# Splitting the blocks of the next down-product later and its weights earlier in a Strassen-scheduled encoder layer

## The chip, the cores and the metric

The kernel runs on one core of a Trainium2 chip. The metric is the device time of one launch in microseconds (us).

## The reference, cut to what matters

One layer of a hybrid streaming encoder (recurrent and gated mixers, output projection, then a gated feed-forward part) over 1024 prompt frames and 64 sample frames, 1088 columns in all. The change lies in the last product of the layer, the down projection of the feed-forward part, and in the normalisation and residual add behind it:

```python
    hn2 = rmsnorm(x, g_pre2)
    up = hn2 @ w_up
    upc, new_ffn = causal_dwconv(up, ffn_prev, w_conv_f, b_conv_f)
    f = (jax.nn.gelu(upc[..., :D_FF]) * upc[..., D_FF:]) @ w_down
    x = x + rmsnorm(f, g_post2)
```

D_MODEL is 1024 and D_FF is 3072. The frames lie along the free axis, the features along the 128 partitions.

## The kernel before

The kernel first runs the mixers, the output projection and the up projection, and spends its last quarter in the down projection. Every matrix product is made of three passes: an operand is split into a high part (written by ACT, `hi`) and a low part (the operand less its high part, by DVE, `lo`), and high by high, high by low and low by high are added up in PSUM. So each operand costs one ACT and one DVE instruction before TensorE can use it.

The down projection is done by a Strassen scheme: seven half-size products (`DOWN`), whose operands are sums of quarters. Each product has six steps (`down_step`, 48 matmuls of 272 columns each), so steps are numbered 0 to 41. Step n needs its own weights (one tile of 128x1024, high and low) and two of the six gated blocks of its product: steps 0 and 3 of a product use blocks 0 and 1, steps 1 and 4 blocks 2 and 3, steps 2 and 5 blocks 4 and 5. A step takes the first of its two blocks at its start and the second a quarter of the step later. I number blocks through, 6 to a product, as `bload` and `bmake` do.

- `bload(b)` (L977) loads a block of 128x1088 from DRAM on the SP queue, as tile `graw`; `bmake(b)` splits it into `gh` (L143, ACT) and `gl` (L145, DVE).
- `wload(n)` (L998) loads the one or two weight quarters of step n on the SP queue, as `wraw`; `wmake(n)` first takes their difference where there are two (L1008, DVE; products 2, 3 and 6, so steps 12 to 23 and 36 to 41) and then splits it into `whi` (L143) and `wlo` (L145).
- `down_step(n)` issues the matmuls (L1069) into PSUM tiles `dps`. In the third step of each half product DVE adds the sums to the accumulators `facc` (L1078), on ACT for the first product (L1086), and for some products their squares are summed (`ssqt`, L221 and L222).
- The last product (steps 36 to 41) is done over two column ranges (`COLS2`, r = 0 and 1), each over all six weight sets, into tiles `lps`. Its first range, as long as three steps, takes the weight sets in turn, half a step's length each; set 41 is first wanted 2.5 steps after its start, and block 41 after 2.15.
- `finish` normalises a finished range of columns: `rstd_head` (matmuls `st`, L196, then L187 on DVE and L188 on POOL), `rstd_tail` (matmuls `bp`, L208, and a copy on ACT), then eight scalings on DVE (L1121). For the first half of the columns the result is added to the residual in DRAM by POOL's DMAs; for the last two ranges the residual is loaded by `load_xn` (L1108, SP queue) and added on DVE (L1126, and L1144 in `finish_last`).

All these tiles but PSUM's come from one pool of 47 buffers of a row of 1096 words. A high or low part can be written only when an earlier tile's readers, mostly matmuls of an earlier step, are done with its buffer. The order of instructions on each engine is fixed when the program is built: the text order above, as a scheduler with priorities places it. Engines and the SP queue work through their rows in that order, so an instruction that waits holds back all rows behind it on its engine.

Of the kernel before, what the change touches and what calls it, by code (L numbers as in the profile page):

```python
# [41 lines left out]
NDS = 6 * len(DOWN)  # L42
# [25 lines left out]
def layer_kernel(ctx: ExitStack, tc, xT, w_fm, w_v, w_o, w_up, w_down, w_g, w_s, par, bc, yT, small, vn_out):  # L68
# [9 lines left out]
    def bank_tile(name):  # L78
        return mmp.tile([P, 512], F32, tag="mm", name=name)
# [3 lines left out]
    def big_tile(dt=F32, shape=(P, TW), name="t"):  # L83
        return big.tile(list(shape), dt, tag="t", name=name)

    def tmp_tile(w, name="d"):
        return tmp.tile([P, 288], F32, tag="d", name=name)[:, :w]
# [54 lines left out]
    def split(hi, lo, src, scale=None):  # L142
        nc.scalar.activation(hi, src, AF.Copy, scale=1.0 if scale is None else scale)  # L143
        if scale is None:
            nc.vector.tensor_tensor(lo, src, hi.bitcast(F32), op=ALU.subtract)  # L145
        else:
            nc.vector.scalar_tensor_tensor(lo, src, scale, hi.bitcast(F32), op0=ALU.mult, op1=ALU.subtract)
# [93 lines left out]
    def pcols(i):  # L241
        return slice(i * PC, min(i * PC + PC, T))
# [71 lines left out]
    for k in range(KD):  # L314
        xh.append(big_tile(F32R, name="xh")[:, :T])
        xl.append(big_tile(F32R, name="xl")[:, :T])
        if k == 0:
# [3 lines left out]
            for i in range(3):  # L321
                n = pcols(i).stop - pcols(i).start
# [12 lines left out]
    for i in range(3):  # L335
        n = pcols(i).stop - pcols(i).start
# [6 lines left out]
    s = [big_tile(name="s")[:, :T] for _ in range(4)]  # L343
# [275 lines left out]
    def run(gen):  # L619
        for _ in gen:  # L620
            pass
# [349 lines left out]
    bq, braw, wq, wraw = {}, {}, {}, {}  # L971
    sd = drp.tile([2, 6, P, 1024], F32, tag="sd", name="sd")

    def bload(n):
        if n < NDS:
            braw[n] = big_tile(name="graw")[:, :T]
            nc.sync.dma_start(braw[n], bd[n // 6, n % 6].rearrange("p a t -> p (a t)"))  # L977

    def bmake(n):
        if n < NDS:  # L980
            bq[n] = big_tile(F32R, name="gh")[:, :T], big_tile(F32R, name="gl")[:, :T]
            split(*bq[n], braw.pop(n))

    def w_index(n):
        i = n % 6
        return i if n < NDS - 6 else i % 2 * 3 + i // 2

    def wload(n):
        if n >= NDS:
            return  # L990
        p, i = n // 6, w_index(n)
        a11, a12, a21, a22 = (w_down[r, c, i] for r in range(2) for c in range(2))
        s1, s2 = sd[0, i], sd[1, i]
        wraw[n] = []
        for src in {"A11": (a11,), "S2": (s1, a11), "S3": (a11, a21), "A22": (a22,), "A12": (a12,),
                    "S1": (s1,), "S4": (a12, s2)}[DOWN[p][1]]:
            t = big_tile(shape=(P, 1024), name="wraw")
            nc.sync.dma_start(t, src)  # L998
            wraw[n].append(t)

    def wmake(n):
        if n >= NDS:
            return
        p, i = n // 6, w_index(n)
        raw = wraw.pop(n)
        src = raw[0]
        if len(raw) == 2:
            nc.vector.tensor_tensor(src, src, raw[1], op=ALU.subtract)  # L1008
        if DOWN[p][1] == "S2":
            nc.gpsimd.dma_start(sd[1, i], src)  # L1010
        wq[n] = big_tile(F32R, (P, 1024), name="whi"), big_tile(F32R, (P, 1024), name="wlo")
        split(*wq[n], src)
# [9 lines left out]
    for j in range(NPRE, NF):  # L1022
# [7 lines left out]
        i = j - NPRE - 2  # L1030
# [9 lines left out]
    late.pop()()  # L1040
    opb.clear()
    wmake(2)
    bmake(5)
    wload(4)
    wmake(3)
    bload(6)

    ssqt = []
    gens2 = []
# [1 line left out]
    def tick2():  # L1051
        if gens2 and next(gens2[0], 0) == 0:
            gens2.pop(0)

    def facc_cols(m, lo, hi):
        return facc[m][:, lo:hi]

    def sq_add(m, lo, hi, eng=None):
        if not ssqt:
            ssqt.append(big_tile(name="ssqt")[:, :T])  # L1060
        add_sq(ssqt[0][:, lo:hi], facc_cols(m, lo, hi), m == (0 if lo < HT else 4), eng)

    def down_mm(dst, cols, n, kg, k, mi, first, last):
        hi, lo = wq[n]
        bh, bl = bq[n // 6 * 6 + kg * 2 + k // 2]
        o = k % 2 * HT
        for q, (wt, at) in enumerate(((hi, bh), (hi, bl), (lo, bh))):
            for ps, (a, b) in zip(dst, cols):
                nc.tensor.matmul(ps, wt[:, k * 256 + mi * P:k * 256 + (mi + 1) * P], at[:, o + a:o + b],  # L1069
                                 start=(first and k == 0 and q == 0), stop=(last and k == 3 and q == 2))  # L1070
# [33 lines left out]
    def load_xn(cols):  # L1104
        w = cols.stop - cols.start
        xn = [big_tile(name="xn")[:, :4 * w].rearrange("p (m t) -> p m t", m=4) for _ in range(2)]
        for g in range(2):
            nc.sync.dma_start(xn[g], yT[:, 4 * g:4 * g + 4, cols])  # L1108
        return xn

    def finish(cols, xn=None):
        w = cols.stop - cols.start
        head = rstd_head(ssqt[0][:, cols], D)
        yield
        yield
        rr = tmp_tile(w, name="rrf")
        rstd_tail(head, rr)
        yield
        for m in range(KD):
            f = facc[m][:, cols]  # L1120
            nc.vector.scalar_tensor_tensor(f, f, pv("g_post2", m), rr, op0=ALU.mult, op1=ALU.mult)  # L1121
            if xn is None:
                nc.gpsimd.dma_start(yT[:, m, cols], f, accum_op=ALU.add)
            else:
                x = xn[m // 4][:, m % 4, :]
                nc.vector.tensor_tensor(x, x, f, op=ALU.add)  # L1126
                if m % 4 == 3:
                    nc.sync.dma_start(yT[:, m - 3:m + 1, cols], xn[m // 4])
            if m % 2 == 1:
                yield  # L1130

    def scale_f(m, cols):
        f = facc[m][:, cols]
        nc.scalar.activation(f, f, AF.Copy, scale=pv("g_post2", m))
# [14 lines left out]
    def down_step(n):  # L1149
        p, mp, kg = n // 6, n % 6 // 3, n % 3  # L1150
        for mi in range(2):
            m = 2 * mp + mi
            if kg == 0:
                dps[m] = [bank_tile("dps")[:, :HC] for _ in CC]
            for k in range(4):
                down_mm(dps[m], CC, n, kg, k, mi, kg == 0, kg == 2)
            if kg == 2:
                down_evac(p, m, dps.pop(m))
            tick2()
        if mp == 1:  # L1160
            for b in range(2):
                del bq[p * 6 + 2 * kg + b]
        del wq[n]

    dps = {}
    n0 = NDS - 6
    for n in range(n0):
        if n == n0 - 6:
            for c in COLS1:
                gens2.append(finish(slice(*c)))  # L1170
        down_step(n)
        wmake(n + 4)
        if n < n0 - 6:
            bmake(n + 6)
            bload(n + 7)
        elif n == n0 - 6:
            bload(n0 + 1)
            bmake(n0)
            bload(n0 + 2)
            bmake(n0 + 1)  # L1180
        elif n < n0 - 1:
            bload(n + 8)
            bmake(n + 7)
        wload(n + 5)
        if n == 0:
            while todo:
                run(todo.pop(0))
        if n == 1:
            nc.gpsimd.dma_start(small, sm)
    wmake(n0 + 4)  # L1190
    wload(n0 + 5)
    for r, (lo, hi) in enumerate(COLS2):
        cols = slice(lo, hi)
        w = hi - lo
        loc = [(lo - HT, hi - HT)]
        xn = load_xn(cols)
        pss = [bank_tile("lps")[:, :w] for _ in range(4)]

        def mm(m, kg):
            for k in range(4):  # L1200
                down_mm([pss[m]], loc, n0 + 2 * kg + m // 2, kg, k, m % 2, kg == 0, kg == 2)
            tick2()

        if r == 0:
            for kg in range(2):
                for m in range(4):
                    mm(m, kg)
                if kg == 0:
                    wmake(n0 + 5)
        else:  # L1210
            for m in range(4, KD):
                scale_f(m, cols)
        for m in range(4):
            for kg in range(2 if r == 0 else 0, 3):
                mm(m, kg)
            f = facc_cols(m, lo, hi)
            with tc.high_priority(offset=PRI):
                nc.vector.tensor_tensor(f, pss[m], f, op=ALU.add)
                if r == 1 and m == 3:
                    more = tmp_tile(w, name="sq")  # L1220
                    nc.scalar.activation(more, f, AF.Square)
                else:
                    sq_add(m, lo, hi)
                    if r == 1:
                        scale_f(m, cols)
        if r == 0:
            gens2.append(finish(cols, xn))
# [80 lines left out]
```

## Time and profile before

| | |
|---|---|
| median of 3 runs | 1160.79 us (1159.71 to 2815.52) |
| the profiled execution's own time | 1158.54 us |
| its span, first to last instruction | 1156.8 us |
| busy: PE, DVE, ACT, POOL | 97%, 73%, 46%, 14% |
| start of the down projection in the span | 866.71 us |

The profiled execution's own time is its span and 1.7 us around it. One of the three runs, at 2815.52 us, is far off the other two. Times in the rows are microseconds from the start of the span; "mean ns of one" is the duration of one instruction.

### The profile page before, as it was taken

The page shows a single profiled execution, that of the slowest core. Times are in us where ns is not written, and L with a number is a line of the kernel's source. Part 1 is how long each engine was busy: PE and PEld are TensorE (multiplying, and loading weights), DVE is VectorE, ACT ScalarE, POOL GpSimd, SP SyncE. Part 2 cuts the span into 40 slices and gives each one's busy share as a digit, 9 for nine tenths or more (in the row PEclk, how much of TensorE's full clock was granted, in tenths as well). Part 3 has the DMA queues.
Part 4 walks back from the last instruction along what each step waited for, and adds up shares of the span by engine and source line. Part 5 has one row for each costly group of instructions (what it writes and reads, how often), then busy time and mean ns, then how long its engine had stood idle before and what let it go on. Part 6 is the DMA issues. An engine that isn't in the chain of part 4 may idle for free.

```text
span 1156.8 us, 20691 instructions
## 1 busy us (share of the span) xinstructions
PE 1125.6 (97%) x8420; PEld 1104.3 (95%) x8420; DVE 845.1 (73%) x1415; ACT 535.3 (46%) x923; POOL 163.3 (14%) x277
## 2 busy tenths in 40 slices
PE   7999999999999999999999999999999998999995
PEld 6799999999998999999999999999999998999885
DVE  7567776856687898887787787887889355744766
ACT  7213846545445546544544544444466232523421
POOL 0210001010000122222112021021022000001310
PEclk9999999999999999999999999999999999999988
DMA  8110111221333125465342142142168689455952
GB/s 317 37 42 19 37 55 37 66 84 53 97 116 117 37 84 159 141 191 125 94 141 95 47 141 95 47 141 95 47 220 324 230 292 331 133 188 180 270 133 78
DMA packets 53615, 148.61 MB, mean 128 GB/s; under 512 B 5520, under 2 KB 23440, under 8 KB 53424
## 3 DMA queue, kind: packets, MB, share of 16 engines
q1 hardware_dynamic: 39648, 114.57, 29.4%
q0 software_dynamic: 13104, 32.04, 9.2%
q8 instruction: 66, 1.08, 0.4%
q10 hardware_dynamic: 768, 0.69, 0.2%
q14 instruction: 29, 0.24, 0.1%
HBM read 111.57 MB, written 41.99 MB: 133 GB/s over the span
## 4 chain that ended last, share of the span: by engine, by line
PE 91%; DVE 5%; issue 2%; ACT 1%; DMA 0%; POOL 0%; SPq 0%; POOLq 0%; DVEq 0%; ACTq 0%
PE up L901 40%; PE dps L1069 17%; PE ps L429 12%; PE ops L654 7%; PE pps L769 4%; PE vps L294 3%; PE lps L1069 3%; PE gps L515 1%; PE bp L208 1%; PE sp L386 1%; ACT whi L143 1%; PE st L196 1%; DVE wraw L1008 1%; DVE gl L145 1%; DVE bl L145 0%
## 5 line engine op out<-in xcount | busy, mean ns | idle before, releaser
L901 PE MATMUL up<-bh,wop 128*128 128x272 f32 x2464 | 466.0, 289 | 0.0
L901 PEld LDWEIGHTS up<-bh,wop 128*128 128x128 f32 x2464 | 386.7, 188 | 2.1 <-ACT uraw L916 1.3
L901 PE MATMUL up<-bl,wop 128*128 128x272 f32 x1232 | 354.8, 288 | 0.0
L901 PEld LDWEIGHTS up<-bl,wop 128*128 128x128 f32 x1232 | 231.9, 188 | 0.0
L1069 PE MATMUL dps<-gh,whi 128*128 128x272 f32 x576 | 120.2, 291 | 3.1 <-ACT whi L143 3.0
L1069 PE MATMUL dps<-gl,whi 128*128 128x272 f32 x576 | 120.6, 290 | 1.6 <-DVE gl L145 1.5
L1069 PE MATMUL dps<-gh,wlo 128*128 128x272 f32 x576 | 120.0, 290 | 0.0
L143 ACT ACTIVATE wop<-wsum 128x512 fp32r<-128x512 f32 x88 | 53.3, 628 | 116.8 <-DVE wsum L857 76.3
L145 DVE TENSOR_TENSOR wlo<-wraw,whi 128x1024 fp32r<-128x1024 f32 x70 | 85.1, 1220 | 27.5 <-ACT whi L143 27.2
L143 ACT ACTIVATE whi<-wraw 128x1024 fp32r<-128x1024 f32 x70 | 73.2, 1055 | 67.7 <-DVE wraw L1008 56.4
L1069 PEld LDWEIGHTS dps<-gh,whi 128*128 128x128 f32 x576 | 91.1, 190 | 3.5 <-ACT whi L143 3.3
L1069 PEld LDWEIGHTS dps<-gl,whi 128*128 128x128 f32 x576 | 91.4, 190 | 2.2 <-DVE gl L145 2.2
L916 ACT ACTIVATE uraw<-up 128x272 f32<-128x272 f32 (+2 forms) x220 | 67.9, 344 | 53.8 <-PE up L901 53.5
L1069 PEld LDWEIGHTS dps<-gh,wlo 128*128 128x128 f32 x576 | 91.2, 190 | 0.1
L801 DVE SCALAR_TENSOR_TENSOR yg<-uraw,pt,yg 128x1090 f32<-128x1090 f32 (+1 forms) x48 | 64.8, 1350 | 26.4 <-ACT yg L799 26.4
L922 DVE TENSOR_TENSOR uraw<-up,uraw 128x272 f32<-128x272 f32 (+2 forms) x176 | 58.8, 364 | 32.2 <-PE up L901 29.9
L654 PE MATMUL ops<-yh,whi 128*128 128x272 f32 x256 | 75.1, 293 | 0.0
L654 PE MATMUL ops<-yh,wlo 128*128 128x272 f32 x256 | 73.7, 288 | 0.0
L654 PE MATMUL ops<-yl,whi 128*128 128x272 f32 x256 | 73.6, 288 | 0.0
L429 PE MATMUL ps<-xh,whi 128*128 128x364 f32 (+2 forms) x296 | 69.4, 328 | 0.0
L188 POOL TENSOR_TENSOR rs<-v,mhalf 91x3 f32<-91x3 f32 (+2 forms) x20 | 24.6, 1229 | 308.2 <-DVE v L187 308.2
L429 PE MATMUL ps<-xh,wlo 128*128 128x364 f32 (+2 forms) x296 | 67.7, 324 | 0.0
(219 smaller groups left out, 2181.6 us busy)
## 6 DMA issues: line engine op xcount, KB each, us to landing
wraw<-in_w_up_dram SPq DMA_DIRECT2D x48, 512.0 KB, 4.1
graw<-bd SPq DMA_DIRECT2D x42, 544.0 KB, 5.5
wraw<-in_w_down_dram SPq DMA_DIRECT2D x42, 512.0 KB, 6.3
bd<-yg POOLq DMA_DIRECT2D x36, 272.0 KB, 3.4
wraw<-sd SPq DMA_DIRECT2D x18, 512.0 KB, 5.9
bd<-ta POOLq DMA_DIRECT2D x24, 272.0 KB, 4.2
bd<-tb POOLq DMA_DIRECT2D x24, 272.0 KB, 3.4
wraw<-in_w_fm_dram SPq DMA_DIRECT2D x12, 512.0 KB, 3.6
```

The source lines that it names most:

```text
L143: nc.scalar.activation(hi, src, AF.Copy, scale=1.0 if scale is None else scale)
L145: nc.vector.tensor_tensor(lo, src, hi.bitcast(F32), op=ALU.subtract)
L188: nc.gpsimd.tensor_tensor(out, v[:n[0], :n[1]], mhalf[:n[0], :n[1]], op=ALU.pow)
L294: nc.tensor.matmul(ps[b][:vrows(b), :], a[:, vcols(b)], wt[:, o:o + 512], start=False, stop=(k == KD - 1 and q == 2))
L429: nc.tensor.matmul(ps[c], wt[:, k * P:(k + 1) * P], at[k][:, cols], start=(k == 0 and q == 0), stop=(k == KD - 1 and q == 2))
L654: nc.tensor.matmul(ps, wt[:, i * 256 + mi * P:i * 256 + (mi + 1) * P], a[k, c], start=(first and i == 0 and j == 0), stop=(last and i == 3 ...
L769: nc.tensor.matmul(ps, wt[:, k * P:(k + 1) * P], a[k, c], start=(k == 0 and j == 0), stop=(k == KD - 1 and j == 2))
L801: nc.vector.scalar_tensor_tensor(y[:, d:TG], x[:, :TG - d], tap(2 - d), y[:, d:TG], op0=ALU.mult, op1=ALU.add)
L901: nc.tensor.matmul(dst[c], wt[:, k * P:(k + 1) * P], at[:, fourth(k)], start=(start and k == 0 and q == 0), stop=(k == 3 and q == 2), skip ...
L916: nc.scalar.activation(d, src[c][:, cut], AF.Copy)
L922: nc.vector.tensor_tensor(d, src[c][:, cut], d, op=ALU.add)
L1069: nc.tensor.matmul(ps, wt[:, k * 256 + mi * P:k * 256 + (mi + 1) * P], at[:, o + a:o + b], start=(first and k == 0 and q == 0), stop=(last ...
```

## The change

The order of loads and splits in the down projection is written anew, in a helper `operands_after(n)` that runs behind each step. Weights of step n + 4 (one or two steps more from step 34 on) are split first, and weights are loaded two steps beyond that, in place of one. Blocks of the next product are no longer split one behind each step, six steps ahead (up to step 29), but by a table `B_MAKE`: none behind the second step of a product (block 6 there stands for the next product's first), block 6 behind its third step, 7 and 8 behind its fourth, 9 behind its fifth, 10 behind its sixth, and the last one behind the first step of the next product. A block is loaded one step before it is split, and behind the weight loads of its step. Before step 0, block 5 is no longer split and block 6 no longer loaded. In the last product the weight splits and the last block splits now stand behind its two first thirds, and the residual load of r = 0 behind these matmuls, in place of ahead of them.

```diff
@@ -1040,10 +1040,8 @@
     wmake(2)
-    bmake(5)
     wload(4)
     wmake(3)
-    bload(6)
@@ -1164,36 +1162,39 @@
+    B_MAKE = {2: (6,), 3: (7, 8), 4: (9,), 5: (10,), 0: (5,)}
+
+    def operands_after(n):
+        made = max(wq)
+        up_to = min(n + 4 + max(0, n - n0 + 4) // 2, NDS - 1)
+        while wloaded[0] < min(up_to + 2, NDS - 1):
+            wloaded[0] += 1
+            wload(wloaded[0])
+        for i in range(made + 1, up_to + 1):
+            wmake(i)
+        s = n % 6
+        for b in B_MAKE.get(s, ()):
+            bmake(n - s + b)
+        for b in B_MAKE.get((s + 1) % 6, ()):
+            bload(n + 1 - (s + 1) % 6 + b)
+
+    wloaded = [4]
     for n in range(n0):
...
         down_step(n)
-        wmake(n + 4)
-        if n < n0 - 6:
-            bmake(n + 6)
-            bload(n + 7)
-        elif n == n0 - 6:
-            bload(n0 + 1)
-            bmake(n0)
-            bload(n0 + 2)
-            bmake(n0 + 1)
-        elif n < n0 - 1:
-            bload(n + 8)
-            bmake(n + 7)
-        wload(n + 5)
+        operands_after(n)
...
-    wmake(n0 + 4)
-    wload(n0 + 5)
     for r, (lo, hi) in enumerate(COLS2):
...
-        xn = load_xn(cols)
+        xn = load_xn(cols) if r else None
...
             for kg in range(2):
                 for m in range(4):
                     mm(m, kg)
-                if kg == 0:
-                    wmake(n0 + 5)
+                operands_after(n0 + kg)
+            xn = load_xn(cols)
```

On DVE around the end of product 2, this is the order before. The first row is the weight difference of step 17, `facc` rows are the sums at the end of step 17, and `wraw_10650` belongs to step 18.

```order
L1008 TENSOR_TENSOR wraw_10586<-wraw_10586,wraw_10588 128x1024
L145 TENSOR_TENSOR wlo_10641<-wraw_10586,whi_10640 128x1024
L145 TENSOR_TENSOR gl_10645<-graw_10584,gh_10644 128x1088
L1078 TENSOR_TENSOR facc_10061<-dps_10721,facc_10061 128x272
L1078 TENSOR_TENSOR facc_10061<-dps_10722,facc_10061 128x272
L1078 TENSOR_TENSOR facc_10090<-dps_10747,facc_10090 128x272
L1078 TENSOR_TENSOR facc_10090<-dps_10748,facc_10090 128x272
L1008 TENSOR_TENSOR wraw_10650<-wraw_10650,wraw_10652 128x1024
L145 TENSOR_TENSOR wlo_10708<-wraw_10650,whi_10707 128x1024
L145 TENSOR_TENSOR gl_10712<-graw_10648,gh_10711 128x1088
```

And now on DVE, `wraw_10572` is step 18 and `wraw_10634` step 19, and the `facc` rows are the sums at the end of step 14.

```order
L1008 TENSOR_TENSOR wraw_10572<-wraw_10572,wraw_10574 128x1024
L145 TENSOR_TENSOR wlo_10641<-wraw_10504,whi_10640 128x1024
L1008 TENSOR_TENSOR wraw_10634<-wraw_10634,wraw_10636 128x1024
L1076 TENSOR_TENSOR facc_9857<-dps_10520,facc_9857 128x272
L1076 TENSOR_TENSOR facc_9857<-dps_10521,facc_9857 128x272
L145 TENSOR_TENSOR wlo_10704<-wraw_10572,whi_10703 128x1024
L1076 TENSOR_TENSOR facc_9886<-dps_10546,facc_9886 128x272
L1076 TENSOR_TENSOR facc_9886<-dps_10547,facc_9886 128x272
L145 TENSOR_TENSOR gl_10708<-graw_10644,gh_10707 128x1088
```

The difference and the split for step 18 moved from behind the sums of step 17 to the sums of step 14, three steps earlier.

On DVE at the start of the last product, this is the order before: the split for step 36 (`wlo_11926`), sums and squares of step 35, six scalings of `finish`, and then the difference for step 37 (`wraw_11935`).

```order
L145 TENSOR_TENSOR wlo_11926<-wraw_11848,whi_11925 128x1024
L1078 TENSOR_TENSOR facc_10090<-dps_11970,facc_10090 128x272
L145 TENSOR_TENSOR gl_11932<-graw_11842,gh_11931 128x1088
L222 TENSOR_TENSOR ssqt_10259<-ssqt_10259,sq_12147 128x272
L222 TENSOR_TENSOR ssqt_10259<-ssqt_10259,sq_12150 128x272
L1121 SCALAR_TENSOR_TENSOR facc_10061<-facc_10061,pt_79,rrf_12113 128x272
L1121 SCALAR_TENSOR_TENSOR facc_10090<-facc_10090,pt_79,rrf_12113 128x272
L1121 SCALAR_TENSOR_TENSOR facc_11070<-facc_11070,pt_79,rrf_12113 128x272
L1121 SCALAR_TENSOR_TENSOR facc_11097<-facc_11097,pt_79,rrf_12113 128x272
L1121 SCALAR_TENSOR_TENSOR facc_11260<-facc_11260,pt_79,rrf_12113 128x272
L1121 SCALAR_TENSOR_TENSOR facc_11287<-facc_11287,pt_79,rrf_12113 128x272
L1008 TENSOR_TENSOR wraw_11935<-wraw_11935,wraw_11937 128x1024
```

And now on DVE the sums in the middle of step 35 (the `facc` rows) come behind the splits for steps 38, 39 and 40 (`wlo_12068`, `wlo_12073`, `wlo_12162`). The row `v` is the second `rstd_head`, which waits for `st` matmuls that now stand in the middle of step 34.

```order
L1008 TENSOR_TENSOR wraw_11983<-wraw_11983,wraw_11985 128x1024
L187 TENSOR_SCALAR v_12031<-st_12026 91x3
L1008 TENSOR_TENSOR wraw_12058<-wraw_12058,wraw_12060 128x1024
L145 TENSOR_TENSOR wlo_12068<-wraw_11910,whi_12067 128x1024
L145 TENSOR_TENSOR wlo_12073<-wraw_11983,whi_12072 128x1024
L145 TENSOR_TENSOR gl_12077<-graw_12000,gh_12076 128x1088
L145 TENSOR_TENSOR wlo_12162<-wraw_12058,whi_12161 128x1024
L1076 TENSOR_TENSOR facc_11256<-dps_11927,facc_11256 128x272
L1076 TENSOR_TENSOR facc_11256<-dps_11928,facc_11256 128x272
```

The splits for steps 36 and 37 moved further up still, ahead of the first `finish`; only the one for step 41 is left behind these rows, after the six scalings.

## Rows read from the trace of the kernel before

**Rows 1.** PE's waits from 820 us on: total us, times, longest.

```profile
PE lps L1069 <- ACT whi L143: 4.6, 2, 2.6
PE dps L1069 <- ACT whi L143: 3.0, 1, 3.0
PE bp L208 <- POOL rs L188: 2.0, 2, 1.4
PE dps L1069 <- DVE gl L145: 1.5, 2, 1.0
```

**Rows 2.** Matmuls of L1069 in 10-us stretches: PE busy (count), PEld, PEclk, DMA share, GB/s.

```profile
890.00:900.00 10.00, 10.00 (x83) 10.00 (x82) 1.00 0.77 277
...
950.00:960.00 10.00, 9.42 (x71) 8.76 (x70) 1.00 0.79 297
970.00:980.00 10.00, 6.96 (x54) 6.75 (x54) 0.93 1.00 378
980.00:990.00 10.00, 10.00 (x61) 9.92 (x61) 0.73 0.35 123
1060.00:1070.00 10.00, 8.28 (x64) 7.69 (x62) 1.00 0.42 85
1090.00:1100.00 10.00, 7.06 (x45) 6.42 (x44) 0.90 0.89 272
1100.00:1110.00 10.00, 7.38 (x40) 7.04 (x39) 0.76 1.13 282
1130.00:1140.00 10.00, 8.26 (x64) 7.88 (x63) 1.00 0.01 2
```

**Rows 3.** The chain of waits from 840 us on: start, us, what.

```profile
866.87 72.06 PE dps L1069 x575
...
977.31 1.14 DVE wraw L1008
...
1057.73 0.41 PE st L196 x6
...
1064.29 0.65 PE bp L208 x6
```

**Rows 4.** Timeline of SP from 944 us: the loads for step 18.

```profile
945.50 2.74 SPq L998 DMA_DIRECT2D wraw<-in_w_down_dram  x2
```

**Rows 5.** The page's DMA issues: KB each, median us to landing.

```profile
wraw<-in_w_down_dram SPq DMA_DIRECT2D x42, 512.0 KB, 6.3
```

**Rows 6.** Timeline of DVE, steps 11 to 14: start, us, [idle before <-releaser].

```profile
935.92 0.79 DVE L1078 TENSOR_TENSOR facc<-dps,facc 128x272 f32<-128x272 f32 x2 [8.52 <-PE dps L1069]
...
940.86 1.49 DVE L222 TENSOR_TENSOR ssqt<-ssqt,sq 128x272 f32<-128x272 f32 x4
...
944.61 1.23 DVE L145 TENSOR_TENSOR wlo<-wraw,whi 128x1024 fp32r<-128x1024 f32 x1 [1.12 <-ACT whi L143]
945.75 1.29 DVE L145 TENSOR_TENSOR gl<-graw,gh 128x1088 fp32r<-128x1088 f32 x1
```

**Rows 7.** Timeline of DVE at the start of the last product.

```profile
1091.26 1.49 DVE L1078 TENSOR_TENSOR facc<-dps,facc 128x272 f32<-128x272 f32 x4 [5.60 <-PE dps L1069]
...
1094.19 1.22 DVE L1008 TENSOR_TENSOR wraw<-wraw 128x1024 f32<-128x1024 f32 x1
...
1099.93 2.56 DVE L1121 SCALAR_TENSOR_TENSOR facc<-facc,pt,rrf 128x272 f32<-128x272 f32 x6
1102.41 1.22 DVE L1008 TENSOR_TENSOR wraw<-wraw 128x1024 f32<-128x1024 f32 x1
```

**Rows 8.** Timeline of ACT in steps 0 and 1: the weight split of step 4.

```profile
874.31 1.06 ACT L143 ACTIVATE whi<-wraw 128x1024 fp32r<-128x1024 f32 x1 [0.17 <-DMA wraw<-in_w_down_dram]
```

**Rows 9.** Timeline of DVE in the tail.

```profile
1147.83 0.44 DVE L1126 TENSOR_TENSOR xn<-xn,facc 128x274 f32<-128x274 f32 x1
```

**Rows 10.** Timeline of POOL: the second and third `rs` of `finish`.

```profile
1070.10 4.21 POOL L188 TENSOR_TENSOR rs<-v,mhalf 91x3 f32<-91x3 f32 x1
...
1135.69 0.88 POOL L188 TENSOR_TENSOR rs<-v,mhalf 92x3 f32<-92x3 f32 x1 [29.69 <-DVE v L187]
```

## Prediction

> **What bounds the kernel now.** I read the waits of PE first, then PE's matmuls in stretches of 10 us, then the chain and the timelines of DVE, ACT and SP around the stops. PE is the engine that sets the end: in an undisturbed stretch of the down projection its matmuls follow each other without a pause, 575 in 72.06 us or 125.3 ns each [rows 3], so a step of 48 takes 6.015 us. The reader is to see where it does not run like that. PE waits for a high part of a weight (`whi`) 4.6 us in the last product and 3.0 us at the start of step 18, and for `gl` 1.5 us [rows 1]. The stretches show what that costs: 82 to 83 matmuls of L1069 in ten undisturbed us, but 71 from 950 us, 54 and 61 from 970, 64 from 1060, 45 and 40 from 1090 and 64 from 1130 [rows 2]. The granted clock falls to 0.73 behind the stop of step 18 and to 0.76 behind those of the last product [rows 2], so part of the time stands at the lower of the two levels, 1.2 in place of 2.4 GHz, although PE has work.
>
> Are late loads the reason? No. The two quarters for step 18 were issued from 945.50 us on [rows 4] and such loads land in a median of 6.3 us [rows 5], so they lay there by about 955; their difference began at 977.31 [rows 3]. DVE came late, by its order: the difference stands behind the sums of step 17, and these wait for PE. DVE idles in front of such sums, 8.52 us at 935.92 [rows 6], with splits queued behind them; later it runs difference, `wlo` and `gl` one by one, with 1.12 us of waiting for ACT in each turn [rows 6]. It is the same in the last product: the difference for step 36 begins at 1094.19, behind the sums of step 35, and that for step 37 at 1102.41, behind six scalings of 2.56 us [rows 7], while PE stands.
>
> **Weights split earlier, step 18.** Now this difference and split stand at the sums of step 14. Without stops step n begins at 866.7 + 6.015 n, so those sums come at about 953 to 957 and step 18 begins at 975.0: about 18 us of room in place of none. The stop and the slow clock behind it go. From 970 us two stretches have 115 matmuls in place of 164: 49 times 0.1253 is 6.1 us.
>
> **Blocks split later.** This frees buffers for the weights, but each block comes nearer to its use, and a late one stops PE as 950 us and 1060 us show: 11 and 18 matmuls missing, 1.4 and 2.3 us, of which 1.06 us in the second are the `st` and `bp` matmuls (0.41 and 0.65 [rows 3]) that stay. I go through the nearest places, by DVE's new order. In product 2 the last block `gl` (for step 14 and a quarter, due at 952.7) stands behind the sums of step 11 (at 938.9 plus 0.8), four additions of squares (1.5), two differences, two `wlo` and two `gl`; these six take 1.14 to 1.28 us each, start to start, if ACT is ahead, which it is with one split of 1.06 us [rows 8] for each. That ends at about 948.3, 4.4 us ahead; with ACT's 1.12 us [rows 6] in each of two turns still 2.2 us ahead. In product 0, block 5 is split behind the weights of steps 3 and 4. Before, step 4's `whi` began at 874.31 as its load landed [rows 8]; then come `wlo`, 1.06 us later, or ACT's `gh` (by its width 1.1 us), and DVE's `gl`, 1.28 us: done at about 877.9, and due at step 2.29, 880.5. That is 2.6 us ahead. Other products have 5 us and more. So I take nothing for new stops here, and nothing left of the old: 1.4 and 2.3 less 1.06 us, or 2.6 us, are won.
>
> **The last product.** Splits for sets 36 to 40 now stand ahead of the sums of step 35, so PE finds them at once. The longest thing left is set 41: behind the start of step 36 DVE has four sums (1.49 [rows 7]), two squares (0.8), a `gl` of 1.28, six scalings (2.56), a difference (1.14), ACT's `whi` with its hand-over (1.15), `wlo` and the last `gl`, 10.9 us in all, and block 41 is due 2.15 steps or 12.9 us behind that start. So 2 us ahead, no stop. From 1090 us the stretches lack 79 of 164 matmuls, 9.9 us, of which a `bp` of 0.65 us stays: 9.25 us. At 1130 us 18 are missing, 2.3 us, of which `st` and `bp` keep 1.06: before, `bp` came so soon behind `st` that PE waited for POOL [rows 1], now half a step lies between. That is 1.2 us.
>
> **Loads.** The weight loads that pass the block loads on SP are worth nothing by themselves, since loads lay 20 us unused (above). Their price is bounded by block loads that come later: these go behind one step's weights, at most two loads, and are issued a step ahead of their split. The residual load of r = 0 stands now behind the last block loads, at about 1080 us, and its data are used behind `finish`, in step 40, some 25 us later. It costs nothing; in the tail, one residual addition of r = 0 that stood among the last sixteen operations (0.44 us, of which 0.35 count [rows 9]) goes.
>
> **The sum.** 6.1 + 2.6 + 9.25 + 1.2 + 0.35 is 19.5 us. Against the profiled execution's own 1158.54 us that is 1139.0. I leave 0.5 us for short waits at `st` and `bp`, which I bound by 0 and by the 2.0 us of [rows 1]. The two near runs stand 1.2 and 2.3 us above the profiled execution, so a median should come at 1139.5 + 1.5, or **1141 us**, 1.7% below 1160.79. There is little to win beyond that: with all these gone PE runs through.
>
> **The rivals.**
> *POOL late.* The second `rs` now falls beside five operations of DVE in a row (a difference, three `wlo`, a `gl`), each with two inputs from SBUF, some 5.9 us. The same operation took 4.21 us at 1070 among DVE work and 0.88 us at 1135.69 with DVE nearly idle [rows 10]. If it waits them all out and then takes 0.88 us, it ends 6.8 us behind `v`, and `bp` is due 5.3 us behind `v`: PE stops for 1.5 us, and the time is 1142.5. For it: the 4.21 us. Against: even 4.21 us would fit. The Trainium skill, SBUF — State Buffer, section "Who interferes with whom", says that "A DVE instruction with two SBUF inputs contends with a GpSimd instruction that reads SBUF"; this is such a pair. By that rule the time would be 1142.5, by the 4.21 us of the row 1141; no run here shows a full wait.
> *One or two stops stay or arise.* A place with 2 to 2.6 us of room (block 5, product 2, block 41) is missed by a few us and drops the clock: each costs 1.4 us at least and 6.1 at most [rows 2], so 1142.5 to 1153, with 1147 as a middle. For it: my room is a sum of durations, and landings of loads vary. Against: three places at most.
> *The change doesn't do what it says.* Buffers, not DVE's order, hold the splits, and the stops only move: 1158 to 1161. Against: the order shows sums and splits in another place, and `wraw` had landed.
> *Slower.* Late blocks stop PE at the start of each product: a product's sixth block is split only behind its first step, 7.5 us (a step and a quarter) ahead of its use. If the splits in front of it take more than that, each of the six later products stops as step 18 did, 6.1 us: 1141 + 36.6 is 1178. It decides where the block's `gl` ends later than 7.5 us behind the end of that first step. Against: in product 2 I count 9.4 us of work from the end of step 11 to the last block, which is due 13.8 us behind that end, and before, blocks came later than that there (the `gl` waits of [rows 1]).
>
> **How the numbers follow.** Chances: 0.70 for the forecast (1137.5 to 1144, with 1141 the likeliest), 0.08 for POOL late, 0.13 for one or two stops, 0.05 for no change, 0.04 for slower. The range goes from 1137.5, the sum with nothing left over and no offset of runs, less 1.5 us, to 1148, which takes in more than half of the third case; some 0.14 is left out. Two per cent, about what a measurement of this kernel can tell from no change, is 23.2 us here: faster than 1137.6 needs more than my whole sum, 0.06; slower than 1184 needs the last rival at its full price and more, 0.01; the rest, 0.93, lies within.
>
> **What would show it.** Right: in the profile after, PE's waits for `whi` and `gl` from 866 us on fall from 9 us to under 1, every stretch of 10 us has 80 or more matmuls until the `st` and `bp` of the end, the granted clock stays at 1.00 until the tail, the difference for step 18 begins near 950 us, and the last matmul of L1069 ends near 1123 us in place of 1142. Wrong: a new wait of PE for `gl` or `gh` at step 2, at steps 12 to 15 or behind step 38, a clock under 0.9 in a stretch, sums that come late so that PE waits for a bank of PSUM, or a tail longer than before.

## The result, and the profile after

The changed kernel takes 1140.46 us (median of 4 runs, 1139.20 to 1140.82) where the kernel before took 1160.53 us on the same chip: a ratio of 0.984, 95% interval 0.982 to 0.985. The forecast was 1141.0 us, in a range of 1137.5 to 1148. Three runs far above the others of their kernel (2815.52 us of the kernel before, 1222.42 and 1825.86 us in two of the experiments) are left out of the ratios. The profiled run after took 1140.82 us; its span is 1138.9 us.

PE's waits from 820 us on, in the changed kernel (total us, times, longest), which answer to [rows 1]:

```profile
PE bp L208 <- POOL rs L188: 1.2, 1, 1.2
PE st L198 <- ACT sq L1222: 0.9, 1, 0.9
```

That is the whole list. The waits for `whi` and `gl`, 9.1 us in [rows 1], are gone, and what is left lies in the tail; the 0.9 us for `st` were there before too, below the rows shown in [rows 1]. The matmuls of the down projection (L1067 now) in the stretches of [rows 2]; the columns are those of [rows 2]:

```profile
890.00:900.00 10.00, 10.00 (x82) 10.00 (x81) 1.00 1.01 359
950.00:960.00 10.00, 10.00 (x82) 10.00 (x81) 1.00 0.89 324
970.00:980.00 10.00, 10.00 (x82) 10.00 (x81) 1.00 0.68 232
980.00:990.00 10.00, 10.00 (x82) 10.00 (x81) 1.00 0.55 192
1060.00:1070.00 10.00, 10.00 (x82) 10.00 (x81) 1.00 0.89 176
1090.00:1100.00 10.00, 10.00 (x81) 10.00 (x80) 1.00 0.74 94
1100.00:1110.00 10.00, 9.45 (x75) 9.25 (x75) 1.00 0.01 2
1110.00:1120.00 10.00, 9.57 (x77) 9.38 (x76) 1.00 0.17 57
1130.00:1140.00 10.00, 0.00 (x0) 0.00 (x0) 0.50 0.31 111
```

The stretches up to 1100 us that lacked matmuls now have 81 or 82, and the granted clock stays at 1.00 until the tail. The stretches at 1100 and 1110 us lack some because the `st` and `bp` matmuls of the `finish` now stand in them. For the same reason three stretches that are not shown, at 1050, 1070 and 1080 us, have 73, 78 and 77, where the prediction wanted 80 in every one until the end. The chain of waits (start, us, what) answers to [rows 3]:

```profile
868.24 183.56 PE dps L1067 x1464
1051.80 0.41 PE st L196 x6
1052.21 6.13 PE dps L1067 x48
1058.33 0.64 PE bp L208 x6
...
1087.33 19.89 PE lps L1067 x156
...
1128.42 1.60 PE bp L208 x6
```

PE runs through in one piece of 183.56 us, 1464 matmuls at 125.4 ns, where the undisturbed piece of [rows 3] had 575. DVE's timeline shows why; it answers to [rows 6] and to the difference at 977.31 in [rows 3]. By the order of the program, the difference at 946.05 is that of step 17 and the one at 949.52 that of step 18:

```profile
946.05 1.22 DVE L1008 TENSOR_TENSOR wraw<-wraw 128x1024 f32<-128x1024 f32 x1
947.19 1.22 DVE L145 TENSOR_TENSOR wlo<-wraw,whi 128x1024 fp32r<-128x1024 f32 x1
948.32 1.29 DVE L145 TENSOR_TENSOR gl<-graw,gh 128x1088 fp32r<-128x1088 f32 x1
949.52 1.22 DVE L1008 TENSOR_TENSOR wraw<-wraw 128x1024 f32<-128x1024 f32 x1
```

The difference for step 18 starts 27.8 us earlier than before and 26.9 us ahead of the step, which begins at 976.40 us. DVE does one operation behind the other, with no wait for ACT in between.

The time by parts of the down projection, from the starts of PE's matmuls in the two traces (us):

| | before | after | won | forecast |
|---|---|---|---|---|
| steps 0 to 11 | 72.17 | 72.16 | 0.0 | 0 |
| steps 12 to 17 | 40.76 | 36.15 | 4.6 | |
| steps 18 to 23 | 38.80 | 36.10 | 2.7 | |
| both products | | | 7.3 | 6.1 + 1.4 |
| steps 24 to 29 | 36.13 | 36.12 | 0.0 | 0 |
| step 30 to the last matmul | 87.57 | 76.32 | 11.25 | 1.2 + 9.25 + 1.2 |
| the tail | 14.63 | 13.95 | 0.7 | 0.35 |

Together 19.25 us, with 19.5 forecast. The profiled run's span shrank by 17.9 only, since this run started the down projection at 868.08 us in place of 866.71. That is no effect of the edit that these runs can tell: the same kernel, run once more (below), started it at 866.92.

### The profile page after: what moved, and what is told of

Read it like the earlier page. It is cut to its first block, busy times and chain, and to the rows that moved or that the text cites. A ratio compares the mean times of both kernels' runs of the same rounds, so it can differ in the third digit from the quotient of the medians.

```text
span 1138.9 us, 20692 instructions
## 1 busy us (share of the span) xinstructions
PE 1118.7 (98%) x8420; PEld 1099.1 (97%) x8420; DVE 844.4 (74%) x1415; ACT 535.8 (47%) x923; POOL 164.5 (14%) x277
## 4 chain that ended last, share of the span: by engine, by line
PE 93%; DVE 3%; issue 2%; DMA 0%; POOL 0%; ACT 0%; SPq 0%; POOLq 0%; DVEq 0%
PE up L901 41%; PE dps L1067 19%; PE ps L429 12%; PE ops L654 7%; PE pps L769 4%; PE vps L294 4%; PE lps L1067 2%; PE gps L515 1%; PE bp L208 1%; PE sp L386 1%; PE st L196 1%; DVE bl L145 0%; DMA wraw<-in_w_v_dram 0%; POOL rs L188 0%; DVE mix L715 0%
## 5 line engine op out<-in xcount | busy, mean ns | idle before, releaser
L1067 PE MATMUL dps<-gh,whi 128*128 128x272 f32 x576 | 119.5, 288 | 0.0
L1067 PE MATMUL dps<-gh,wlo 128*128 128x272 f32 x576 | 119.2, 288 | 0.0
L1067 PE MATMUL dps<-gl,whi 128*128 128x272 f32 x576 | 119.1, 288 | 0.0
L1067 PEld LDWEIGHTS dps<-gh,wlo 128*128 128x128 f32 x576 | 90.4, 188 | 0.0
L1067 PEld LDWEIGHTS dps<-gh,whi 128*128 128x128 f32 x576 | 90.4, 188 | 0.0
L1067 PEld LDWEIGHTS dps<-gl,whi 128*128 128x128 f32 x576 | 90.3, 188 | 0.0
```

## The experiments

The number was right. The question is whether its reasons were. The prediction held that DVE's order stopped PE (the **order** part), that the later block splits free the buffers which let the weight splits move up (the **buffer** part), and that the earlier weight loads are worth nothing by themselves. The rival that I put against it: the weight loads alone change the order, and the blocks are worth nothing. Medians are in us; the ratio is to the kernel before on the same chip, with its 95% interval.

### Loads two steps ahead, alone

The kernel before with:

```diff
+        if n == 0:
+            wload(5)
-        wload(n + 5)
+        wload(n + 6)
```

and without the `wload(n0 + 5)` ahead of the last product.

> The kernel before with one edit: weights are loaded two steps beyond the step that is split, in place of one; blocks, load order within a step and the residual load stay. The prediction's theory (buffers freed by the later block splits let the weight splits move up, loads are worth nothing by themselves) expects the stops of step 18 and of the last product to stay: 1155 to 1161 us. The rival (the scheduler puts a difference where it takes its load to have landed, so earlier loads alone pull differences ahead of the sums) expects 1140 to 1148 us, with the difference for step 18 before 960 us of the span.

Measured: 1140.2, ratio 0.984 (0.982 to 0.986). PE's waits are the two lines of the changed kernel. So the later block splits aren't needed: with all blocks split as early as before, the whole gain is there. The difference for step 18 starts at 961.0 us, 16 us earlier than before and still 16 us ahead of its step, which begins at 977.1; the rival had expected it before 960.

```profile
961.01 1.22 DVE L1008 TENSOR_TENSOR wraw<-wraw 128x1024 f32<-128x1024 f32 x1
```

### Blocks later, alone

The kernel before with the table `B_MAKE` for its blocks (and without the early block 5 and 6), its weights untouched.

> The kernel before with the block table alone (blocks of the next product loaded and split later, block 5 no longer split before step 0); weights are loaded and split as before. The prediction's theory (buffers) expects most of the gain: 1141 to 1150 us. The rival (loads) expects that nothing is won, 1155 to 1161 us, with the difference for step 18 still behind the sums of step 17 and PE waiting there for whi.

Measured: 1160.0, ratio 1.002 (1.001 to 1.004): nothing is won. PE's waits (total, times, longest), the four longest:

```profile
PE lps L1067 <- ACT whi L143: 6.5, 1, 6.5
PE dps L1067 <- ACT gh L143: 3.2, 3, 2.0
PE dps L1067 <- DVE gl L145: 2.3, 4, 0.7
PE bp L208 <- POOL rs L188: 1.7, 2, 1.2
```

The rival's time is right, one detail of it isn't. The difference for step 18 starts at 968.38, ahead of the sums of step 17 and 9.3 us ahead of its step, so the block table alone changes DVE's order there too:

```profile
968.38 1.22 DVE L1008 TENSOR_TENSOR wraw<-wraw 128x1024 f32<-128x1024 f32 x1
974.75 0.79 DVE L1076 TENSOR_TENSOR facc<-dps,facc 128x272 f32<-128x272 f32 x2 [5.14 <-PE dps L1067]
```

PE no longer waits for `whi` at step 18. Instead it stops in products 2 and 3 for the blocks' `gh` and `gl`, 5.3 us in all, and in product 5 for a `wlo`, 1.1 us. This profiled execution took 1156.72 us, the fastest of the ten, so its rows show less than the median's loss. The stop of the last product is the old one: the difference for step 37 stands behind seven scalings, as in [rows 7].

```profile
1096.99 2.98 DVE L1119 SCALAR_TENSOR_TENSOR facc<-facc,pt,rrf 128x272 f32<-128x272 f32 x7
1099.87 1.22 DVE L1008 TENSOR_TENSOR wraw<-wraw 128x1024 f32<-128x1024 f32 x1
```

### The two counter-tests in the changed kernel

Blocks early again: `operands_after` keeps its weights and loads, and its block lines are those of the kernel before.

```diff
-        for b in B_MAKE.get(s, ()):
-            bmake(n - s + b)
-        for b in B_MAKE.get((s + 1) % 6, ()):
-            bload(n + 1 - (s + 1) % 6 + b)
+        if n < n0 - 6:
+            bmake(n + 6)
+            bload(n + 7)
...
```

> The changed kernel with the blocks loaded and split as before (one a step, six steps ahead); weight loads two steps ahead and in front of the block loads, extra weights from step 34 on and the late residual load stay. The prediction's theory (buffers) expects stops at the starts of products: 1150 to 1161 us. The rival (loads) expects 1140 to 1146 us.

Loads one step ahead again, and behind the block loads:

```diff
-        while wloaded[0] < min(up_to + 2, NDS - 1):
+        while wloaded[0] < up_to:
...
+        while wloaded[0] < min(up_to + 1, NDS - 1):
+            wloaded[0] += 1
+            wload(wloaded[0])
```

> The changed kernel with the weight loads put back: one step ahead of the split in place of two, and behind the block loads of their step; block table, extra weights from step 34 on and the late residual load stay. The prediction's theory (loads are worth nothing) expects 1140 to 1143 us. The rival (loads set the order) expects 1152 to 1161 us, with the stop at step 18 back.

Measured: 1144.4 with the blocks early (ratio 0.987, 0.986 to 0.989), 1161.7 with the loads one ahead (1.002, 1.000 to 1.003). Without the loads the changed kernel is worth nothing; without the block table it keeps three quarters of the gain. For the 4 us that it loses PE waits for no block and no weight, but for `rs`: it is the rival "POOL late", with a late weight load behind it (below). With the loads one ahead, PE's longest waits are those of the kernel with the late blocks alone.

### The order alone, with no load moved

The sums of the down projection are tied to their place in the text, where they had a priority over it. Nothing else is changed in the kernel before.

```diff
-                with tc.high_priority(offset=PRI):
-                    nc.vector.tensor_tensor(facc_cols(d, dh * HT + a, dh * HT + b), ps[c],
-                                            facc_cols(s, sh * HT + a, sh * HT + b), op=ALU.add)
+                tc.keep_in_program_order(
+                    nc.vector.tensor_tensor(facc_cols(d, dh * HT + a, dh * HT + b), ps[c],
+                                            facc_cols(s, sh * HT + a, sh * HT + b), op=ALU.add))
```

> The kernel before with loads, blocks and residual load untouched; only the sums of the down projection are tied to their place in the text on DVE, so the difference for step 18 stands ahead of the sums of step 17 as its text does. If the order on DVE is the cause and loads count only through the order that the scheduler writes, the stop of step 18 goes and most of the gain is there without any earlier load: 1140 to 1150 us. If the loads themselves must land earlier, nothing is won: 1155 to 1161 us.

Measured: 1143.0, ratio 0.987 (0.985 to 0.989). Four fifths of the gain without an earlier load. SP and DVE around step 18 in this kernel (start, us, [idle before <-releaser]): the loads of step 18, the sums of step 14, and the difference for step 18:

```profile
940.82 2.42 SPq L998 DMA_DIRECT2D wraw<-in_w_down_dram  x2
```

```profile
957.93 0.79 DVE L1078 TENSOR_TENSOR facc<-dps,facc 128x272 f32<-128x272 f32 x2 [0.59 <-PE dps L1069]
958.64 1.22 DVE L1008 TENSOR_TENSOR wraw<-wraw 128x1024 f32<-128x1024 f32 x1
```

By the trace these two loads landed at 955.1 and 956.3 us, 3 us later than the 952.1 and 953.4 of the kernel before. Yet the difference starts 18.7 us earlier and PE doesn't stop at step 18. So it is DVE's order and not the landing that stopped PE. What it doesn't reach of the changed kernel lies in the last two products and the tail: PE waits three times for `rs`, 3.0 us in all, and 0.5 us each for a `wlo` and for one of the tied sums.

### One difference put back

The changed kernel, where the difference for step 18 and the split that needs it are made behind step 17, and the difference is tied there. Its load stays.

```diff
         for i in range(made + 1, up_to + 1):
-            wmake(i)
+            if i != 18:
+                wmake(i)
+        if n == 17:
+            wmake(18)
...
+            if n == 18:
+                tc.keep_in_program_order(sub)
```

> The changed kernel with one weight difference, that of step 18, tied behind the sums of step 17 on DVE; its load stays where it is, some 35 us earlier. If the order on DVE is the cause, PE stops for 2 to 4 us at step 18 and loses about 6 us with the clock, as before the change: 1145 to 1148 us. If the landing of the load decides, it stays at 1140 us.

Measured: 1146.2, ratio 0.989 (0.987 to 0.992). Its second quarter landed at 941.2 us, 37 us ahead of the difference at 978.5. PE's waits, and the stretch behind them:

```profile
PE dps L1069 <- ACT whi L143: 4.2, 1, 4.2
...
PE dps L1069 <- DVE wlo L145: 0.4, 1, 0.4
```

```profile
980.00:990.00 10.00, 8.72 (x56) 8.50 (x57) 0.83 0.63 213
```

Steps 12 to 23 are longer than in the changed kernel by 40.49 + 38.09 - 36.15 - 36.10 = 6.3 us: 4.6 of waiting, for `whi` and for the `wlo` of the same set, and the rest at a granted clock of 0.83 in the stretch, in which PE works part of the time at the lower of its two levels (1.2 and 2.4 GHz). That is the 6.1 us that the prediction put on this stop, made again with one instruction.

### POOL late, seen

In the changed kernel with early blocks the second `rs` of `finish` stands beside five operations of DVE in a row. PE's wait, POOL's row, DVE's rows, and the stretch of PE:

```profile
PE bp L208 <- POOL rs L188: 4.1, 2, 2.8
```

```profile
1079.80 6.40 POOL L188 TENSOR_TENSOR rs<-v,mhalf 91x3 f32<-91x3 f32 x1 [12.52 <-DVE v L187]
```

```profile
1078.43 1.23 DVE L1008 TENSOR_TENSOR wraw<-wraw 128x1024 f32<-128x1024 f32 x1 [4.74 <-DMA wraw<-sd]
1079.57 0.15 DVE L187 TENSOR_SCALAR v<-st 91x3 f32<-91x3 f32 x1
1079.64 2.35 DVE L145 TENSOR_TENSOR wlo<-wraw,whi 128x1024 fp32r<-128x1024 f32 x2
1081.91 1.28 DVE L145 TENSOR_TENSOR gl<-graw,gh 128x1088 fp32r<-128x1088 f32 x1
1083.11 1.22 DVE L145 TENSOR_TENSOR wlo<-wraw,whi 128x1024 fp32r<-128x1024 f32 x1
1084.25 1.21 DVE L1008 TENSOR_TENSOR wraw<-wraw 128x1024 f32<-128x1024 f32 x1
```

```profile
1080.00:1090.00 10.00, 6.50 (x42) 6.30 (x41) 0.86 0.74 224
```

The five end at 1085.46; 0.88 us more [rows 10] is 1086.34, and `rs` ends at 1086.20. It waited all of them out, as the rival had it.

The first row is what the rival hadn't: the difference for step 40 stands ahead of `v`, and its second quarter landed only at 1078.30 us. DVE waited 4.74 us for it, and `v` started 2.8 us behind the first of the `st` matmuls (1076.75), where it started 0.6 us behind it in the changed kernel. So `rs` ended 6.6 us behind `v` (6.8 in the rival's sum), but `bp` was due only 3.9 us behind `v` (5.3). Here a load did land late.

Steps 30 to 35 take 43.09 us in place of 38.55: 4.5 us, 2.8 of them waiting and the rest at a clock of 0.86. The rival's price of 1.5 us was too low by 1.3 us of waiting, for the late `v`, and by 1.7 us, for the clock.

### The smallest edit that holds the gain

The kernel before with its weight load in front of the splits and the block load of its step, still one step ahead. On SP each weight load passes one block load.

```diff
         down_step(n)
+        wload(n + 5)
         wmake(n + 4)
...
-        wload(n + 5)
```

> The kernel before with the one weight load of each step put in front of that step's weight split and block split and load, still one step ahead of its split. The scheduler's order of DVE then reads like that of two steps ahead, so if that order is what counts: 1140 to 1148 us. If the load must be two steps ahead: 1152 to 1161 us.

> The kernel before with the weight load of each step in front, again and in more rounds. If this one line holds the whole gain, it stands within 1.5 us of the changed kernel on the same chip, 1138 to 1142 us. If the block table, the second step of look-ahead or the residual load are worth something, it is 2 us or more slower than the changed kernel.

Measured: 1138.9 both times (ratio 0.983, 0.981 to 0.985, and 0.983, 0.981 to 0.984). The changed kernel once more, beside the second of these:

> The changed kernel once more, unchanged, as the yardstick for the three others on the same chip: 1139 to 1142 us.

Measured: 1138.9 (ratio 0.983, 0.981 to 0.985).

So one moved line has the whole gain, and the other edits add nothing that these runs can tell. DVE's order in it, around step 18 (`wraw_10638`; the `facc` rows are the sums of step 14):

```
L1008 TENSOR_TENSOR wraw_10574<-wraw_10574,wraw_10576 128x1024
L145 TENSOR_TENSOR wlo_10645<-wraw_10574,whi_10644 128x1024
L1078 TENSOR_TENSOR facc_9867<-dps_10522,facc_9867 128x272
L1078 TENSOR_TENSOR facc_9867<-dps_10523,facc_9867 128x272
L145 TENSOR_TENSOR gl_10649<-graw_10588,gh_10648 128x1088
L1008 TENSOR_TENSOR wraw_10638<-wraw_10638,wraw_10640 128x1024
```

In the kernel before, the same difference stood behind the sums of step 17, three steps later. The text has it behind step 14 in both. A load that stands one place earlier in the text moved the place that the scheduler gives to the instruction that needs it. In the trace it starts here:

```profile
956.39 1.22 DVE L1008 TENSOR_TENSOR wraw<-wraw 128x1024 f32<-128x1024 f32 x1
```

### Blocks later still, the extra sets, the residual load

The changed kernel with all splits and loads of the next product's blocks one step later:

```diff
-    B_MAKE = {2: (6,), 3: (7, 8), 4: (9,), 5: (10,), 0: (5,)}
+    B_MAKE = {3: (6,), 4: (7, 8), 5: (9,), 0: (4,), 1: (5,)}
...
-            bmake(n - s + b)
+            if n - s + b > 4:
+                bmake(n - s + b)
```

> The changed kernel with the blocks of the next product loaded and split one step later still: the sixth block of a product is split behind its second step, a quarter of a step and a step of PE work ahead of its use. The prediction's rival on the slower side (late blocks stop PE in each product and the clock falls) expects a stop of 1 to 4 us at the third step of most products and 1150 to 1185 us. If DVE runs ahead of PE there, 1140 to 1143 us.

Measured: 1141.4, ratio 0.985 (0.984 to 0.987). No wait for a block; the waits of PE are again the two of the changed kernel. The prediction's rival on the slower side would need more than a step of further delay.

The changed kernel without the extra sets: `up_to = min(n + 4 + (n >= n0 - 1), NDS - 1)`.

> The changed kernel without the additional weights from step 34 on: the set for step 40 is split behind step 35 and that for step 41 behind the first third of the last product, as before the change. The prediction's own steps took the extra sets as part of the 9.25 us of the last product, which expects some of these to come back: 1143 to 1150 us. If the order of DVE alone counts, and it is the same here but for the set of step 40, 1139 to 1142 us.

Measured: 1139.1, ratio 0.983 (0.981 to 0.985). They are worth nothing.

The kernel before with only the residual load moved behind the first range's matmuls:

> The kernel before with the residual load of the last product's first range moved behind its matmuls, nothing else. The prediction took it as worth nothing by itself: 1157 to 1160 us, as before. If the load in front of the weight loads held them up on SP, some of the 9.25 us of the last product goes: 1149 to 1155 us.

Measured: 1158.0, ratio 1.000 (0.999 to 1.001). Nothing, as the prediction had it.

## Why the prediction was right, and where it wasn't

**Step 18, 6.1 us: right, and shown.** One difference put back behind the sums of step 17 costs 6.3 us again, though its load lay there; the order changed alone wins it, though the loads landed later.

**Waits for `gl`, 2.6 us, the last product, 9.25 us, and the `bp`, 1.2 us: right.** Products 2 and 3 together gave 7.3 us with 7.5 forecast, the stretch from step 30 on 11.25 with 11.65. The three narrow places held with the room that was counted, within 0.5 us: `gl` of block 5 was done at 879.40, 2.5 us ahead (2.6 forecast), product 2's last block at 949.61, 4.4 us ahead (4.4), block 41 at 1097.80, 2.5 us ahead (2).

**"This frees buffers for the weights": wrong as the cause of the gain.** The block table alone wins nothing (1160.0), and the kernel before with its loads two steps ahead, all blocks early, wins all (1140.2). The table does move the difference for step 18 ahead of the sums (968.38), whether by buffers or not was not tried; but with the loads as before its blocks come late, 5.3 us of stops in products 2 and 3, where the prediction took nothing for new stops. The table is what the largest part of the diff is about, and I took it for the cause because it is.

**"The weight loads that pass the block loads on SP are worth nothing by themselves": wrong in what follows.** This is the step that failed: a term put at nothing that holds the whole gain, 1158 to 1139 us. That the loads lay 20 us unused was read rightly, and from it follows that in the kernel before the difference for step 18 didn't wait for its landing. It doesn't follow that moving them changes nothing: the order of DVE is written when the program is built, and it changed with the loads. One load moved ahead within its step wins 1.7%. Why the scheduler places the difference there (that it reckons with the load's landing would fit) was not tried by itself and stays an argument; what is shown is that the time follows the place of the loads and not that of the blocks. The order by itself follows both.

The number did not come out by luck, but it is no test of these two steps either: its terms were read from the waits before and from DVE's new order as it was built, whichever edit had made that order.

**The residual load, 0: right. The tail, 0.35 us: right in kind,** 0.7 us measured from the last matmul to the end. It comes with the order too: the kernel with the one moved line has the same tail (13.95 us) and loads the residual early, and the kernel with only the residual load moved keeps the old one (14.61). The size can't be told, since the changed kernel run once more has a tail of 13.26 us.

**The rivals.** "Buffers, not DVE's order, hold the splits" fell. "Slower" fell at one step of further delay. "POOL late" did not happen in the changed kernel, where the second `rs` took 1.83 us beside the same kind of operations, but it is real: in the changed kernel an edit of the block lines alone called it up, at three times its price.

## What to carry to other kernels

When the order of instructions is made by a scheduler, ask of an edit first what it does to the order of the engine that feeds the bound one, and take its parts one by one: here a load moved by one place held the whole gain, and the largest part of the diff held none. An operand whose load has long landed can still be late, because its preparation is queued behind work that waits for the engine that it should feed. To tell the two apart, tie the waiting work to its place and leave the loads alone.

## What the runs showed of the hardware

The wait of a small POOL operation beside DVE varies much in like surroundings. In the changed kernel both `rs` stand beside rows of `wlo`, differences and `gl` without a pause on DVE:

```profile
1052.68 5.26 POOL L188 TENSOR_TENSOR rs<-v,mhalf 91x3 f32<-91x3 f32 x1 [104.58 <-DVE v L187]
...
1077.80 1.83 POOL L188 TENSOR_TENSOR rs<-v,mhalf 91x3 f32<-91x3 f32 x1 [10.40 <-DVE v L187]
```

```profile
1077.67 1.23 DVE L1008 TENSOR_TENSOR wraw<-wraw 128x1024 f32<-128x1024 f32 x1
1078.81 2.35 DVE L145 TENSOR_TENSOR wlo<-wraw,whi 128x1024 fp32r<-128x1024 f32 x2
```

The first ends 0.75 us behind the four operations beside it, so it waited them out. The second ends at 1079.63, 0.73 us behind the first of the five operations beside it (1078.90) and with the next one running, so it waited out one. With 6.40 us above that is a range of 1.83 to 6.40 us for 0.88 us of work. The Trainium skill, SBUF — State Buffer, section "Who interferes with whom", says that such a pair contends; all three durations agree, and the 1.83 us shows that POOL can come in between two operations of DVE. What decides after which of them was not tried.

Not every stop of PE costs clock as well. Behind waits of 4.2 and 2.8 us in one piece the granted clock of the stretch fell to 0.83 and 0.86. In the kernel with late blocks alone, PE stood still in several shorter pieces, of 2 us at most, and the stretches stayed at 1.00. But the length of the pieces alone does not decide it: the changed kernel with the loads one ahead has the same two waits in its stretch at 980 us, 1.0 us for `gh` and 0.7 us for `gl`, and there the granted clock fell to 0.83 (last row). What makes the difference stays open.

```profile
940.00:950.00 10.00, 7.34 (x57) 6.90 (x56) 1.00 0.83 256
980.00:990.00 10.00, 8.25 (x63) 7.82 (x63) 1.00 0.71 248
```

```profile
980.00:990.00 10.00, 8.25 (x52) 7.82 (x52) 0.83 0.53 180
```
